# Moving four modulations of a hybrid encoder layer from the first FFN to the mLSTM, with DRAM parking and earlier query-weight loads

## The chip, the cores and the metric

One core of one Trainium2 chip runs the whole layer as a single program. The metric is the device time of one execution in microseconds; of several runs the median counts. TensorE (PE), VectorE (DVE), ScalarE (ACT), GpSimd (POOL) and SyncE (SP) work from queues of their own, in order; SP issues all DMA.

## The reference, cut to what matters

A layer of 1024 tokens by 1024 channels in float32, batch 1: FFN 1, a token mixer, FFN 2, each followed by a residual and a layer norm. A condition vector `c` gives nine modulation vectors of 1024 (shift, scale and gate for each of the three sub-layers; j = 3 * sub-layer + 0, 1, 2).

```python
mod = (silu(c) @ w_ada + b_ada).reshape(bsz, 3, 3, D_MODEL)
f1 = swiglu(modulate(x, mod[:, 0, 0], mod[:, 0, 1]), ffn1_w_up, ffn1_w_down)
x = post_norm(x, 0.5 * f1, mod[:, 0, 2], ln1_g, ln1_b)
tm = token_mixer(modulate(x, mod[:, 1, 0], mod[:, 1, 1]), ...)
x = post_norm(x, tm, mod[:, 1, 2], ln2_g, ln2_b)
f2 = swiglu(modulate(x, mod[:, 2, 0], mod[:, 2, 1]), ffn2_w_up, ffn2_w_down)
x = post_norm(x, 0.5 * f2, mod[:, 2, 2], ln3_g, ln3_b)
```

The mixer projects the tokens to queries, keys, values, output gates, input and forget gates (mLSTM, 4 heads, both directions, chunks of 128 tokens) and to the channels of an S5 state-space model. The mLSTM output is multiplied by the sigmoid of the output gate and normalised per head; the S5 output goes through a gated linear unit; one output projection takes both. So modulations 0 and 1 are needed at once, 2 at the end of FFN 1, 3 and 4 when the first norm is applied, 5 when the output projection is added to the residual, 6 and 7 at the norm after it, and 8 at the end of FFN 2.

## The kernel before

Activations lie channels by tokens, in tiles of 128x512: token half `h`, channel block `k`. All tiles come from a pool of 99 buffers named `s`; PSUM has 8 banks named `b`. Large products are made of three matmuls on operands split into a rounded and a remaining part (`mm3`, line 37); each split costs a cast and a subtraction. The FFN products use a scheme of seven block products, whose operands are combined on VectorE (`pair_jobs`, `product_jobs`), with the hidden rows kept in the DRAM tensors `Td`.

The order of work is made by a planner in Python while the program is built. Main work is a list of jobs on TensorE (`run_jobs`, line 602), whose weights come through a stream that loads up to ten chunks ahead (`Stream`, line 240). Everything else runs in lanes (line 371): generators that put operations into queues of 24, from which `issue` (line 540) takes whatever is ready by the planner's own clock, lanes in a fixed order, the lane `bg` last; each lane leaves some tiles of the pool free. A tile is taken when the operation that first writes it is issued, and a DMA into a tile is an operation like others. All DMAs go to SP's one queue, in the order in which they were planned.

Work around the change:

- `ada` (line 637) makes modulations from `w_ada`: for each j four steps of four loads of 256 KB, fetched a step ahead, and 16 products with 32-column weights (`cpad`), a copy of 256 columns, and for each two steps column sums with the vector `one`. Each of these float32 products leaves two records in the trace. j = 1 at the start is made on VectorE and ScalarE instead.
- `background` in `run` (line 2321), the lane `bg`: modulation 2, then 3 to 8, then the vectors that follow from them (`affine`, `cols`), then `s5_gen` (line 1380), which makes the S5 tables on VectorE and stores them to `Wd`, `Vd`, `Md` and last `Ed` (lines 1677 to 1695).
- `in_jobs` (line 1701): input projection; the last jobs are the values and the output gates, tokens by columns, into tiles of 128x4x128 (line 1775 for the gates, eight tiles that stay in the pool).
- `gates` (line 1829) makes the gate sequences of both directions, writes the running maxima to `Mr` (line 1890) and the query weights to `Wr` (line 1922).
- `mlstm` (line 2132), lane `lv`: for four pairs of chunks it loads `Mr` spread over 128 partitions (`load_m`, line 2149; a pair ahead), makes masked exponentials, and multiplies them with query-key products.
- `direction` (line 2195), lanes `l0` and `l1`: the chunk recurrence in each direction. Before chunk 1 and chunk 4 of a direction two loads of `Wr`, spread over partitions, come directly before the products that use them (lines 2204 to 2211).
- `finalize` (line 2268), lanes `fin0` to `fin3`: output gate (Tanh), per-head norm, transposes, for one chunk.
- `down_jobs` (line 957) in `mixer` (line 2300): the output projection in two halves of the rows, first the S5 channels in four passes of four units, then the mLSTM channels in passes of 8, 6 and 2. A unit is one 128x512 tile of the output; `fetch` loads the residual tiles `R` from `Xd` at the first half, and `evacuate` (line 1009) adds to them with the gate column `gcol[1]`. The 16 residual tiles stay in the pool between the halves.

Of the kernel before, what the change touches and what calls it, by code (L numbers as in the profile page):

```python
# [239 lines left out]
class Stream:  # L240
# [120 lines left out]
    def ensure(self, c):  # L361
        while self.ns <= min(c + AHEAD_SPLIT, len(self.chunks) - 1):
# [12 lines left out]
WINDOW = 24  # L375
U, Q = ("u0", "u1", "u2", "u3"), ("q2", "q3", "q0", "q1")
IN_ORDER = ([(x, 0) for x in U + ("g", "q2")] + [(x, 1) for x in U + ("g", "q2")]
# [18 lines left out]
class Kern:  # L396
    def __init__(self, ctx, tc, I, O, phases=("ffn1", "mixer", "ffn2")):
# [40 lines left out]
        self.Yd = dr.tile([4, 8, 16, 8, 128], F32, name="Yd")  # L438
        self.Mr = dr.tile([2, 4, S], F32, name="Mr")
        self.Wr = dr.tile([2, 4, S], F32, name="Wr")  # L440
# [515 lines left out]

    def down_jobs(self, w, rows, x, sub, passes, drain=(), after=None, fetch=None):

# [17 lines left out]
        for pi, units in enumerate(passes):  # L976
# [3 lines left out]
            for i, kt in enumerate(rows):  # L980
# [6 lines left out]
                def run(i=i, units=units, banks=banks, ys=ys, last=last, pi=pi):  # L987
                    if i == 0:
                        self.room(len(units))
                        banks.update({un: self.bank() for un in units})  # L990
                        if fetch:
                            for un in units:
                                fetch(*un)
                    ws = {y: st.get(idx[i, y]) for y in ys}
                    for un in units:
                        k, hh = un
                        wh, wl = ws[k // 4]
                        cc = slice(k % 4 * 128, k % 4 * 128 + 128)
                        mm3(nc, banks[un], wh[:, cc], wl[:, cc], *hsp[i, hh], i == 0, i == n - 1)
                        yield  # L1000
                    for hh in last:
                        del hsp[i, hh]
                    if i == n - 1:
                        self.later("ev", self.evacuate(sub, units, banks, after, pi))
                    yield

                self.jobs.append(Job(len(st.chunks) - 1, run, drain if pi == 0 and i == 0 else (), pre(i, sorted(new))))

    def evacuate(self, sub, units, banks, after, pi):
        for k, h in units:  # L1010
            self.add_to(sub, k, h, banks[k, h])
            self.free(banks[k, h])
            yield
        if after:
            after(pi)
# [685 lines left out]
    def in_jobs(self, drains):  # L1701
# [53 lines left out]
        def t_job(wi, h, k, c, banks):  # L1755
            def run():
# [10 lines left out]
                if k == KD - 1:  # L1767
                    for t in range(4):
                        if wi == 0:
                            x = self.S([128, 4, 129])  # L1770
                            P.memset(x[:, :, 128:129], 1.0)
                            self.v1[4 * h + t] = x
                            x = x[:, :, :128]
                        else:
                            x = self.o[4 * h + t] = self.S([128, 4, 128])
                        V.tensor_tensor(x, banks[t].rearrange("p (h x) -> p h x", h=4),
                                        bvo[wi].rearrange("p (h x) -> p h x", h=4), op=OP.add)
                    self.free(*banks)
                    if h:
# [49 lines left out]
    def gates(self):  # L1829
# [58 lines left out]
        for d in range(2):  # L1888
            for h in range(2):
                nc.sync.dma_start(self.Mr[d, :, h * 512:(h + 1) * 512], gm[h][RW[d]])  # L1890
        V.tensor_tensor(dc, mm, me, op=OP.subtract)
# [240 lines left out]
    def mlstm(self):  # L2132
# [16 lines left out]
        def load_m(c):  # L2149
            r = []  # L2150
            for d in range(2):
                mr = self.S([128, 4, 128])
                nc.sync.dma_start(mr, self.bc_ap(self.Mr, d * 4 * S + c * 128, [[0, 128], [S, 4], [1, 128]]))
                r.append(mr)
# [40 lines left out]
    def direction(self, d):  # L2195
# [3 lines left out]
        C = self.S([128, 2, 129])  # L2199
        qs = {}  # L2200
        for j in range(8):
            c = j if d == 0 else 7 - j
            hc, ts = self.tok(c)
            if j in (1, 4):
                for a in range(2):
                    x = qs[a] = self.S()
                    nc.sync.dma_start(x, self.bc_ap(self.Wr, (d * 4 + 2 * a) * S + hc * 512,
                                                    [[S, 2], [0, 64], [1, 512]]))
                    nc.any.tensor_tensor(x, x, qk[a, hc], op=OP.mult)
                del x  # L2210
                yield
            yield from self.wait(("vis", c))
            self.mark(("dir", d, j))
# [54 lines left out]
    def finalize(self, c):  # L2268
# [3 lines left out]
        while c not in self.o:  # L2272
            yield
        x, o, ng = self.cell.pop(c), self.o.pop(c), self.v["mlstm_norm_g"]
        nc.scalar.activation(o, o, AF.Tanh, scale=0.5)
# [24 lines left out]
    def mixer(self):  # L2300
# [8 lines left out]
        for n, first in enumerate((4, 0) if S5_FIRST else (0, 4)):  # L2309
            self.down_jobs(I["w_out"], range(first, first + 4), lambda i, h, f=first: self.rows(f + i, h), 1,  # L2310
                           self.END if n else self.QUARTERS, lanes[first == 0],
                           self.post(1, "ln2_g", "ln2_b", 2) if n else None, None if n else lambda k, h: self.fetch(self.Xd, k, h))

    def run(self):
# [6 lines left out]
        def background():  # L2321
# [3 lines left out]
            self.mark(("cols", 0))  # L2325
            yield from self.ada(range(3, 9))
            self.cpad = None
            self.affine(1, "ln1_g", "ln1_b")
            self.cols(1, False)
            self.affine(2, *(("ln2_g", "ln2_b") if mixer else ("ln1_g", "ln1_b")))  # L2330
            self.cols(2, True)
            for x in (("affine", 1), ("affine", 2), ("cols", 1), ("cols", 2)):
                self.mark(x)
            if mixer:
                yield from self.s5_gen()
                self.mark(("tables",))

# [91 lines left out]
```

## Time and profile before

| | us |
|---|---|
| Median of 3 runs | 1940.88 |
| Lowest and highest run | 1940.76, 1946.27 |
| Profiled execution, its own time | 1939.65 |
| Its span, first to last instruction | 1937.9 |
| TensorE busy in the span | 1847.2 |
| VectorE busy in the span | 1600.0 |
| ScalarE busy in the span | 648.2 |
| Mean granted TensorE clock, share of full speed | 0.982 |

Every operation is recorded at the helper's line 79, so groups are told apart by operation, tile and shape. In order of time: modulations and the first products (to about 165 us), the up products of FFN 1, its down products and the first norm (to about 820 us), input projection and S5 (to about 980 us), gated unit and mLSTM, the output projection's two halves (to about 1282 us), FFN 2.

### The profile page before, as it was taken

What the parts mean: (1) busy time and instruction counts of PE and PEld (TensorE: products, weight loads), DVE (VectorE), ACT (ScalarE), POOL (GpSimd) and SP (SyncE); (2) the same over time, 40 slices, a digit from 0 to 9 for tenths busy, and PEclk for the clock granted to TensorE, in tenths of its full rate; (3) what the DMA queues carried; (4) which work ended last, traced back from release to release, by engine and by line L of the source; (5) the groups of instructions that cost most, each with busy time, mean ns of one, the idle gap of its engine ahead of it and who ended that gap; (6) DMA issues with size and microseconds to landing.
All of it is one profiled execution on the core that took longest, in us unless ns stands there. A gap on an engine that the chain in (4) does not pass through costs nothing.

```text
span 1937.9 us, 29643 instructions
## 1 busy us (share of the span) xinstructions
PE 1847.2 (95%) x10544; PEld 1455.7 (75%) x10544; DVE 1600.0 (83%) x3351; ACT 648.2 (33%) x1201; POOL 200.6 (10%) x203
## 2 busy tenths in 40 slices
PE   5999999999999899999998899999999999999996
PEld 4767888777788677777776677678888888887775
DVE  7937889989899999879986796998677767597887
ACT  4512333333332326522253432542222222233412
POOL 0000000000000001110112311301111211000014
PEclk9999999999999989999999899999999999999998
DMA  9985233434493735482633430223232323574512
GB/s 325 313 300 192 82 110 116 158 132 141 150 343 113 262 129 196 159 271 73 207 104 93 150 97 11 77 91 121 84 121 95 109 82 109 179 256 143 184 44 76
DMA packets 187331, 290.54 MB, mean 150 GB/s; under 512 B 27024, under 2 KB 54800, under 8 KB 187184
## 3 DMA queue, kind: packets, MB, share of 16 engines
q1 hardware_dynamic: 187184, 288.65, 44.6%
q8 instruction: 83, 1.36, 0.3%
q14 instruction: 64, 0.52, 0.1%
HBM read 218.26 MB, written 70.32 MB: 149 GB/s over the span
## 4 chain that ended last, share of the span: by engine, by line
PE 79%; DVE 11%; DMA 5%; issue 3%; ACT 1%; SPq 0%; POOL 0%; DVEq 0%; ACTq 0%; POOLq 0%
PE b L79 79%; DVE s L79 10%; DMA s<-in_w_ada 2%; ACT s L79 1%; DMA s<-Wr 1%; DMA s<-in_x 1%; DVE er L79 0%; SPq L79 0%; DMA s<-in_glu_w 0%; DMA s<-in_w_first 0%; DVE lnv L79 0%; DMA s<-in_w_down 0%; DMA s<-Md 0%; DMA s<-Td 0%; POOL s L79 0%
## 5 line engine op out<-in xcount | busy, mean ns | idle before, releaser
L79 PE MATMUL b<-s 128*128 128x512 f32 (+5 forms) x9208 | 1817.6, 372 | 55.8 <-DVE s L79 37.1
L79 PEld LDWEIGHTS b<-s 128*128 128x128 f32 (+3 forms) x9208 | 1414.2, 176 | 428.2 <-DVE s L79 55.2
L79 DVE TENSOR_TENSOR s<-s 128x512 fp32r<-128x512 f32 (+5 forms) x1787 | 1003.0, 607 | 77.9 <-ACT s L79 23.6
L79 ACT ACTIVATE s<-s 128x512 fp32r<-128x512 f32 (+3 forms) x676 | 395.6, 625 | 567.3 <-DVE s L79 385.8
L79 DVE TENSOR_TENSOR s<-s,b 128x512 f32<-128x512 f32 (+1 forms) x340 | 215.4, 651 | 176.0 <-PE b L79 170.2
L79 POOL TENSOR_TENSOR s<-s 128x512 f32<-128x512 f32 (+1 forms) x116 | 170.6, 1485 | 1159.6 <-ACT s L79 478.1
L79 ACT ACTIVATE s<-b 128x512 f32<-128x512 f32 (+3 forms) x219 | 119.5, 553 | 479.9 <-PE b L79 446.2
L79 DVE CAST s<-s 128x512 fp32r<-128x512 f32 (+1 forms) x243 | 124.7, 516 | 8.5 <-DMA s<-in_x 3.1
L79 DVE SCALAR_TENSOR_TENSOR s<-b,gcol,s 128x512 f32<-128x512 f32 x56 | 39.5, 744 | 21.9 <-PE b L79 21.9
L79 ACT ACTIVATE s<-b,vec 128x128 f32<-128x128 f32 (+3 forms) x58 | 23.7, 464 | 94.2 <-PE b L79 81.5
L79 POOL MEMSET s<- 128x4 f32 (+3 forms) x57 | 6.0, 131 | 419.0 <-PE b L79 263.6
L79 PE MATMUL b<-ident,s 128*128 128x128 f32 (+1 forms) x208 | 31.5, 279 | 5.2 <-DVE s L79 5.2
L79 PEld LDWEIGHTS b<-ident,s 128*128 128x128 f32 (+1 forms) x208 | 24.9, 149 | 13.5 <-issue 7.7
L79 DVE TENSOR_TENSOR_SCAN s<-s 4x128 f32<-4x128 f32 (+1 forms) x48 | 32.9, 697 | 1.5 <-ACT s L79 0.9
L79 DVE SCALAR_TENSOR_TENSOR s<-s 128x320 f32<-128x320 f32 (+3 forms) x43 | 22.4, 529 | 4.1 <-ACT s L79 3.7
L79 ACT ACTIVATE s<-s,Bp,Gp 128x512 f32<-128x512 f32 x24 | 18.4, 803 | 20.6 <-DVE s L79 20.6
L79 ACT ACTIVATE s<-s,vec 128x512 f32<-128x512 f32 x28 | 20.9, 777 | 11.2 <-DVE s L79 11.1
L79 DVE SCALAR_TENSOR_TENSOR s<-s,vec 128x512 f32<-128x512 f32 (+1 forms) x36 | 24.1, 696 | 0.1
L79 ACT ACTIVATE s<-s,gcols 128x128 f32<-128x128 f32 x64 | 20.0, 391 | 2.7 <-POOL s L79 2.7
L79 PEld LDWEIGHTS b<-one,s 128*32 128x32 f32 x576 | 8.4, 113 | 15.8 <-DVE s L79 12.3
L79 PE MATMUL b<-one,s 128*32 128x1 f32 x576 | 9.2, 174 | 11.5 <-DVE s L79 11.5
L79 DVE SCALAR_TENSOR_TENSOR s<-s,gcol 128x512 f32<-128x512 f32 x24 | 18.8, 783 | 0.6
(102 smaller groups left out, 327.0 us busy)
## 6 DMA issues: line engine op xcount, KB each, us to landing
s<-in_w_up SPq DMA_DIRECT2D x170, 256.0 KB
s<-in_w_ada SPq DMA_DIRECT2D x144, 256.0 KB
Td<-s SPq DMA_DIRECT2D x140, 256.0 KB
s<-Td SPq DMA_DIRECT2D x140, 256.0 KB
s<-in_w_down SPq DMA_DIRECT2D x124, 256.0 KB
s<-in_x SPq DMA_DIRECT2D x32, 256.0 KB
Xd<-s SPq DMA_DIRECT2D x32, 256.0 KB
s<-in_w_vo SPq DMA_DIRECT2D x32, 256.0 KB
```

Of the source, the lines that this page charges most:

```text
L79: self.eng, self.alts, self.emit = eng, (), lambda: getattr(real, name)(*args, **kw)
```

## The change

It makes modulations 2, 3 and 4 as before, then the affine vectors of the first norm and the S5 tables, and modulations 5 to 8 only when the last S5 block (`("y", 7)`) has been made. Output gates are stored to a DRAM tensor `Od` and loaded again by `finalize`. After the first half of the output projection each residual tile is stored to `Xd` and given back; the second half fetches it again. The first two `Wr` loads of each direction are issued when its lane starts, the next two in its third step, ahead of their use in the fifth. `Mr` is laid out chunk by chunk, so that one partition reads 512 numbers in a row. The core of the diff:

```diff
+LATE = ("y", 7)
-        self.Mr = dr.tile([2, 4, S], F32, name="Mr")
+        self.Od = dr.tile([8, 128, 4, 128], F32, name="Od")
+        self.Mr = dr.tile([2, 8, 4, 128], F32, name="Mr")
...
-    def evacuate(self, sub, units, banks, after, pi):
+    def evacuate(self, sub, units, banks, after, pi, store):
         for k, h in units:
             self.add_to(sub, k, h, banks[k, h])
             self.free(banks[k, h])
+            if store:
+                self.nc.sync.dma_start(self.Xd[k * 128:(k + 1) * 128, h * HT:(h + 1) * HT], self.R[k][h])
+                self.R[k][h] = None
             yield
...
-                            x = self.o[4 * h + t] = self.S([128, 4, 128])
+                            x = self.S([128, 4, 128])
                         V.tensor_tensor(x, banks[t].rearrange("p (h x) -> p h x", h=4),
                                         bvo[wi].rearrange("p (h x) -> p h x", h=4), op=OP.add)
+                        if wi:
+                            nc.sync.dma_start(self.Od[4 * h + t], x)
+                            self.o[4 * h + t] = True
...
-                nc.sync.dma_start(self.Mr[d, :, h * 512:(h + 1) * 512], gm[h][RW[d]])
+                nc.sync.dma_start(self.Mr[d, 4 * h:4 * h + 4].rearrange("c h t -> h c t"),
+                                  gm[h][RW[d]].rearrange("h (c t) -> h c t", c=4))
...
-                nc.sync.dma_start(mr, self.bc_ap(self.Mr, d * 4 * S + c * 128, [[0, 128], [S, 4], [1, 128]]))
+                nc.sync.dma_start(mr, self.bc_ap(self.Mr, (d * 8 + c) * 512, [[0, 128], [128, 4], [1, 128]]))
...
-        qs = {}
+        qs, wr = {}, []
+
+        def load_w(hc):
+            for a in range(2):
+                wr.append(self.S())
+                nc.sync.dma_start(wr[a], self.bc_ap(self.Wr, (d * 4 + 2 * a) * S + hc * 512, [[S, 2], [0, 64], [1, 512]]))
+
+        load_w(d)
+        yield
         for j in range(8):
             c = j if d == 0 else 7 - j
             hc, ts = self.tok(c)
             if j in (1, 4):
                 for a in range(2):
-                    x = qs[a] = self.S()
-                    nc.sync.dma_start(x, self.bc_ap(self.Wr, (d * 4 + 2 * a) * S + hc * 512,
-                                                    [[S, 2], [0, 64], [1, 512]]))
-                    nc.any.tensor_tensor(x, x, qk[a, hc], op=OP.mult)
-                del x
+                    qs[a] = wr.pop(0)
+                    nc.any.tensor_tensor(qs[a], qs[a], qk[a, hc], op=OP.mult)
                 yield
+            if j == 2:
+                load_w(1 - d)
...
-        x, o, ng = self.cell.pop(c), self.o.pop(c), self.v["mlstm_norm_g"]
+        x, o, ng = self.cell.pop(c), self.S([128, 4, 128]), self.v["mlstm_norm_g"]
+        nc.sync.dma_start(o, self.Od[c])
         nc.scalar.activation(o, o, AF.Tanh, scale=0.5)
...
-                           self.post(1, "ln2_g", "ln2_b", 2) if n else None, None if n else lambda k, h: self.fetch(self.Xd, k, h))
+                           self.post(1, "ln2_g", "ln2_b", 2) if n else None, lambda k, h: self.fetch(self.Xd, k, h), not n)
...
-            yield from self.ada(range(3, 9))
+            yield from self.ada([3, 4])
+            self.affine(1, "ln1_g", "ln1_b")
+            self.mark(("affine", 1))
+            if mixer:
+                yield from self.s5_gen()
+                self.mark(("tables",))
+                yield from self.wait(LATE)
+            yield from self.ada(range(5, 9))
             self.cpad = None
-            self.affine(1, "ln1_g", "ln1_b")
             self.cols(1, False)
             self.affine(2, *(("ln2_g", "ln2_b") if mixer else ("ln1_g", "ln1_b")))
             self.cols(2, True)
-            for x in (("affine", 1), ("affine", 2), ("cols", 1), ("cols", 2)):
+            for x in (("affine", 2), ("cols", 1), ("cols", 2)):
                 self.mark(x)
-            if mixer:
-                yield from self.s5_gen()
-                self.mark(("tables",))
```

## Rows read from the trace of the kernel before

**Rows 1.** The page's first table, busy time by engine.

```profile
PE 1847.2 (95%) x10544; PEld 1455.7 (75%) x10544; DVE 1600.0 (83%) x3351; ACT 648.2 (33%) x1201; POOL 200.6 (10%) x203
```

**Rows 2.** The chain of waits, whole span: start us, us, what.

```profile
153.47 502.29 PE b L79 x2503
...
1053.98 19.44 DMA s<-Wr
```

**Rows 3.** Windows, FFN 1: us, PE, PEld, DVE, ACT, POOL, clock, DMA share, GB/s.

```profile
60.00:160.00 100.00, 97.97 (x1538) 68.86 (x1531) 58.60 (x112) 29.75 (x61) 7.21 (x4) 1.00 0.88 307
104.00:154.00 50.00, 47.97 (x717) 33.89 (x716) 10.35 (x18) 10.28 (x23) 2.98 (x2) 1.00 0.93 329
165.00:655.00 490.00, 490.00 (x2339) 390.77 (x2338) 447.01 (x1031) 162.86 (x289) 6.40 (x19) 1.00 0.46 153
655.00:680.00 25.00, 17.34 (x71) 13.63 (x70) 24.30 (x41) 7.35 (x12) 0.00 (x0) 0.91 0.81 286
```

**Rows 4.** Windows, mixer, columns as in rows 3.

```profile
976.00:1054.00 78.00, 77.53 (x380) 61.54 (x379) 64.24 (x110) 39.26 (x75) 19.86 (x19) 1.00 0.41 111
1054.00:1078.00 24.00, 11.14 (x51) 7.90 (x49) 8.49 (x29) 5.07 (x17) 0.00 (x0) 0.79 0.36 113
1078.00:1117.00 39.00, 35.18 (x292) 27.68 (x291) 35.80 (x121) 21.26 (x66) 16.45 (x17) 0.91 0.49 150
1117.00:1182.00 65.00, 61.58 (x341) 48.05 (x340) 59.62 (x294) 22.93 (x61) 6.22 (x6) 1.00 0.24 74
```

**Rows 5.** Groups by shape, whole span: busy us, mean ns, idle before.

```profile
L79 PE MATMUL b<-s 128*32 128x128 f32 x1024 | 40.1, 278 | 2.4 <-DMA s<-in_w_ada 1.9 <-issue 0.4
...
L79 DVE TENSOR_TENSOR s<-s,b 128x256 f32<-128x256 f32 x32 | 12.0, 410 | 0.0
```

**Rows 6.** Groups by shape, PE, 60 to 160 us.

```profile
L79 PE MATMUL b<-s 128*128 128x512 f32 x242 | 66.9, 412 | 0.0
L79 PE MATMUL b<-s 128*32 128x128 f32 x880 | 33.8, 278 | 2.0 <-DMA s<-in_w_ada 1.9
L79 PE MATMUL b<-one,s 128*32 128x1 f32 x416 | 5.8, 172 | 0.0
```

**Rows 7.** Groups by shape, PE, 170 to 300 us.

```profile
L79 PE MATMUL b<-s 128*128 128x512 f32 x562 | 130.5, 394 | 0.0
```

**Rows 8.** Timeline of SP's queue, a late store of the tables.

```profile
744.15 0.32 SPq L79 DMA_DIRECT2D Ed<-s  x1
```

**Rows 9.** Timeline of PE, FFN 1's down products, idle before in brackets.

```profile
677.60 32.94 PE L79 MATMUL b<-s 128*128 128x512 f32 x132 [7.66 <-DVE s L79]
715.30 11.75 PE L79 MATMUL b<-s 128*128 128x512 f32 x41 [4.76 <-DVE s L79]
```

**Rows 10.** Timeline of PE, a burst of modulation products.

```profile
141.34 0.43 PE L79 MATMUL b<-s 128*32 128x128 f32 x8 [0.45 <-DMA s<-in_w_ada]
```

**Rows 11.** Timeline of DVE, mLSTM, idle before in brackets.

```profile
1056.90 1.29 DVE L79 TENSOR_TENSOR s<-s 128x512 f32<-128x512 f32 x2 [8.06 <-DMA s<-Wr]
...
1062.11 0.69 DVE L79 TENSOR_TENSOR s<-s 128x512 f32<-128x512 f32 x1 [3.64 <-DMA s<-Wr]
...
1073.44 1.29 DVE L79 TENSOR_TENSOR s<-s 128x512 f32<-128x512 f32 x2 [8.86 <-DMA s<-Wr]
```

**Rows 12.** Timeline of SP's queue, mLSTM.

```profile
1006.35 23.20 SPq L79 DMA_DIRECT2D s<-in_w_out  x4
1031.54 11.65 SPq L79 DMA_DIRECT2D s<-Mr  x8
...
1047.56 1.19 SPq L79 DMA_DIRECT2D s<-Wr  x2
...
1053.37 5.80 SPq L79 DMA_DIRECT2D s<-Wr  x2
```

**Rows 13.** Windows of 5 us, mLSTM, columns as in rows 3.

```profile
1040.00:1045.00 5.00, 5.00 (x28) 3.89 (x27) 4.96 (x5) 2.73 (x6) 5.00 (x4) 1.00 0.86 208
1080.00:1085.00 5.00, 5.00 (x28) 4.14 (x28) 4.93 (x10) 0.28 (x1) 5.00 (x5) 0.51 0.48 125
```

**Rows 14.** Waits, whole span: total us, times, longest us.

```profile
ACT s L79 <- DMA s<-Td: 76.9, 34, 13.7
```

More of the change, by code (lines that the diff above doesn't have):

```diff
@@ L954, in pair_jobs, with down_jobs @@
             self.jobs.append(Job(cs[p], job(p), (("t", sub),) if f == NPLAIN[sub] and p == 0 else ()))
-    def down_jobs(self, w, rows, x, sub, passes, drain=(), after=None, fetch=None):
+    def down_jobs(self, w, rows, x, sub, passes, drain=(), after=None, fetch=None, store=False):
         nc, st = self.nc, self.st
@@ L1003, in run @@
                     if i == n - 1:
-                        self.later("ev", self.evacuate(sub, units, banks, after, pi))
+                        self.later("ev", self.evacuate(sub, units, banks, after, pi, store))
                     yield
                 self.jobs.append(Job(len(st.chunks) - 1, run, drain if pi == 0 and i == 0 else (), pre(i, sorted(new))))
-    def evacuate(self, sub, units, banks, after, pi):
+    def evacuate(self, sub, units, banks, after, pi, store):
         for k, h in units:
```

## The prediction

> **What bounds the kernel now.** I read the page's first table, then the chain of work that ended last, then windows by stage. The reader is to see that TensorE is busy for 1847.2 of 1937.9 us [rows 1]: whatever saves time must take TensorE work away from a stage that is full, or close one of the few gaps. The chain shows both kinds [rows 2]. From 153 us it stays on TensorE for 502.29 us, in the first FFN; near 1054 us it leaves TensorE for 19.44 us, to a load of `Wr` in the mLSTM.
>
> The windows say what each stage has to spare [rows 3]. From 60 to 160 us, where the modulations j = 2 to 8 run beside the first FFN products, PE is busy 97.97 of 100 us, and DMA at 0.88. From 165 to 655 us PE is busy all 490 us while VectorE is at 447.01. So in the first FFN each microsecond of modulation work on TensorE is a microsecond of the program.
>
> In the mixer [rows 4] the stretch from 976 to 1054 us is again full (77.53 of 78), 1054 to 1078 is half empty (11.14 of 24, clock 0.79), and the next two stretches lack 3.8 and 3.4 us. The sum is made against the profiled execution, 1939.65 us (1937.9 of span and 1.75 around it); the median of the runs, 1940.88, stands 1.23 above, and that is added at the end.
>
> **1. Four modulations leave the first FFN.** All 1024 records of the 32-column products belong to eight modulations (j = 0 and 2 to 8), 128 to each [rows 5]. Between 60 and 160 us there are 880 of them, their 416 column sums, and 242 records of 512 columns [rows 6]. What one of these 512-column records takes without company is 130 us / 562 = 0.231 us [rows 7], so the 242 account for 56.0 of 97.97 us, and 42.0 us are the price of 880/128 = 6.9 modulations: 6.1 us each, 24.4 for four. The 2.0 us that PE idled ahead of these records, 1.9 of it for `w_ada` [rows 6], go too.
>
> Does the stream use this time? Its cover would be gone if VectorE couldn't prepare the operands sooner, but from 104 to 154 us VectorE works 10.35 of 50 us [rows 3]. The 64 loads of 256 KB leave the same stretch, where DMA stands at 0.93, so weights don't come later. Modulations j = 2 to 4 stay. I take **-26.4** (between -20, if the stream now and then waits for its own operands, and -26.4).
>
> **2. The S5 tables start earlier.** Their generator ran behind all modulations in the same lane; now it follows j = 4. Its last products, those stored to `Ed`, run on until 744 us [rows 8], in a stretch where VectorE is the bound: 24.30 of 25 us busy from 655 to 680 [rows 3], and PE idles 7.66 and 4.76 us for it [rows 9]. The start moves by about four sevenths of 100 us, 57 us, and the FFN loses 26, so the generator gains some 30 us of lead, not 110: some of the table work leaves this stretch, not all. Between 0 and -12.4; I take **-5**, nearer to the end where VectorE stays full, since it is full here for its own work as well.
>
> **3. The same modulations arrive beside the mLSTM.** They wait for the last S5 block (its output goes out at 976 us) and must be through before the first output-projection results are scaled, for these read `gcol[1]`. Their instructions all count again: 512 product records, 256 column-sum records, 16 copies of 128x256 on ScalarE or VectorE, 64 DMAs on SP's queue.
>
> TensorE's price lies between two rows. In company it was 24.4 us. Eight product records that stand alone take 0.43 us [rows 10], a first one of 0.28 and seven more at 0.022; 128 at that rate and 64 column sums at 5.8/416 = 0.014 [rows 6] make 3.7 us, 14.7 for four, and if they also fill the 7.2 us of gaps left between 1078 and 1182 us, 7.5 remain. The company is 512-column work as before, so I take the first, less 4 us of gaps: **+20.4** (7.5 to 24.4). The copies are put on ScalarE or VectorE; a 128x256 operation took VectorE 0.41 us [rows 5], and ScalarE, busy 39.26 of 78 us there [rows 4], covers 16 of them.
>
> **4. The `Wr` wait.** VectorE, an in-order queue, stands 8.06, 3.64 and 8.86 us for these loads [rows 11]; queued behind are state updates, denominators and masks of both directions, so TensorE runs out. SP issued the loads at 1047.56 and 1053.37 us, the `Mr` loads at 1031.54, after it had been held for 23.20 us in four `w_out` loads [rows 12]. The change issues the first four `Wr` loads when the direction lanes open, and the other four two steps ahead. What is lost now: 12.86 us of PE idle in 1054 to 1078 us, and clock: 11.14 us at 0.79 and 35.18 us at 0.91 lose 2.3 and 3.2 us [rows 4]; TensorE had idled, and was granted 0.51 from 1080 to 1085 us, practically its 1.2 GHz level [rows 13]. Together 18.4. Bounds: 0, if the load still comes last, and -20.6, VectorE's whole wait. I take **-16**: the masks and denominators come next on VectorE, 35.80 of 39 us busy right after.
>
> `Mr` by chunk turns each partition's four runs of 512 bytes into one of 2 KB. Its loads are issued a pair ahead; no engine waits on `Mr` in the trace, so 0 in the sum, between 0 and -4. From 1040 to 1045 us, with `Mr` loads under way, DMA moved 208 GB/s at a share of 0.86, against 329 at 0.93 from 104 to 154 us [rows 3, 13]. The Trainium skill (DMA: Bandwidth & Descriptors, Specifications) puts line rate at runs of 512 bytes and up, by which the new order would move nothing; the rows speak against it in part, since these loads share the stretch with others. By the rule the term is 0, by the rows up to 4 us of earlier masks.
>
> **5. Parking.** Output gates: 8 stores and 8 loads of 256 KB; residual: 16 and 16. A gate's load is issued when its finalize step starts, and Tanh on ScalarE waits for it, with everything behind it. The nearest row is ScalarE's wait for `Td` loads, 76.9/34 = 2.26 us each [rows 14]: 18 us for eight. From 1117 to 1182 us ScalarE is busy 22.93 of 65, TensorE has the first half of the output projection to do [rows 4], so this is covered but for the last step or two: **+2** (0 to 18). The second fetch of the residual is issued when the second half opens and is wanted 96 matmuls, 22 us, later: 0. If SP were held, its cover would be gone and the adds would come late by the load's few microseconds. Stores wait for VectorE's add on SP, with FFN 2 weights behind them: 0, since SP has nothing due before them in that stretch, where DMA is at 0.24 [rows 4].
>
> **The sum:** -26.4 - 5 + 20.4 - 16 + 2 = -25.0; 1939.65 - 25.0 + 1.23 = **1916 us**.
>
> **Rivals.**
>
> *A, slower: SP's single queue.* The place is 976 to 1117 us. SP issues in order, and it has stood for 23.20 us on loads that wanted a free tile [rows 12]. If a modulation load waits so, `Mr` and `Wr` stand behind it. Eight loads in flight, 2.1 MB, take 6.4 us at the 329 GB/s of [rows 3]; once for each of four chunk pairs 25.6 us. With no gain at `Wr` and TensorE's full price: -26.4 + 24.4 + 25.6 = +23.6, 1964 us. It decides from 2 us a pair. The Trainium skill (DMA: Bandwidth & Descriptors, Anatomy of one DMA) has it that a semaphore wait happens on the issuing sequencer, before dispatch; by that rule every new parked store and every load without a tile holds what follows it. For it: 112 more issues in this stage. Against it: DMA at 0.41 and 0.36 [rows 4], so 16.8 MB fit in, and eight gate tiles come free. Chance 0.08.
>
> *B, no change.* The stage takes the modulations at full price, VectorE's chain replaces most of the `Wr` wait, tables give nothing: -26.4 + 24.4 - 4 + 4 (parking) = -2, 1939 us. For it speaks VectorE's load after 1078 us. Chance 0.10.
>
> *C, the loads aren't earlier.* The change wouldn't do what it says: the `Wr` loads stand on SP behind the same `w_out` loads. Everything but term 4 holds: -9, 1932 us. Chance 0.12.
>
> *D, it fits into the gaps.* Modulations +7.5, `Wr` -20.6, tables -12.4: -51.9, 1889 us. Against it: most gaps go with the `Wr` wait. Chance 0.12.
>
> **How the numbers follow.** The forecast has 0.58. Forecast, C and D are faster by over 0.3% (some 6 us, about what a measurement of this kernel can tell from no change): 0.82. B is the same, 0.10; A slower, 0.08. The range runs from 1896, which leaves out most of D, to 1940, which takes in B and C and leaves out A. The bounds of terms 3 to 5 lie within it unless several fall on one side.
>
> **What would show it.** No 32-column products of j = 5 to 8 before 165 us, and the TensorE-only piece of the first FFN over some 26 us sooner; `Ed` stores over well before 700 us; no wait of VectorE for `Wr` over 1 us; 976 us to the start of the output projection's second half (206 us now) within some 8 us of that in spite of 24 us more work. Wrong: waits of TensorE for `w_ada` or of ScalarE for `Od` of several microseconds each, or a clock under 0.9 between 976 and 1182 us.

## The result: 28 us slower, and where it went

The changed kernel takes 1969.34 us (median of 4 runs, 1964.66 to 1974.48) against 1941.04 (4 runs) of the kernel before: ratio 1.0136, 95% interval 1.0117 to 1.0155. The forecast, 1916 us and faster, was wrong, also in sign. The profiled run took 1968.95 us, its span 1967.1.

Three milestones that both traces have split the difference: the last `Xd` store of FFN 1, the last `Yd` store of S5, and the start of TensorE's long piece in FFN 2 on the chain.

| stretch | before, us | after, us | change | forecast |
|---|---|---|---|---|
| start to the last `Xd` store of FFN 1 | 820.4 | 783.7 | -36.7 | -31.4 |
| to the last S5 output store | 155.5 | 160.7 | +5.2 | 0 |
| to FFN 2's long TensorE piece | 305.2 | 367.3 | +62.1 | +6.4 |
| to the end | 656.8 | 655.4 | -1.4 | 0 |
| sum | 1937.9 | 1967.1 | +29.2 | -25.0 |

The rows behind the milestones, the kernel before and then the kernel after (stores on SP with first and last start; the chain's piece):

```profile
L79 SPq DMA_DIRECT2D Xd<-s x16: 319/327/412, 768.8 to 820.4; - x16
L79 SPq DMA_DIRECT2D Yd<-s x8: 320/323/364, 847.4 to 975.9; - x8
1281.13 498.55 PE b L79 x2149
```

```profile
L79 SPq DMA_DIRECT2D Xd<-s x16: 319/327/531, 733.4 to 783.7; - x16
L79 SPq DMA_DIRECT2D Yd<-s x8: 320/323/327, 815.5 to 944.4; - x8
1311.71 497.79 PE b L79 x2149
```

The first stretch came out as forecast, and a little better; the third took 62 us more, all of that gain and 25 us besides. The first table of the page answers to [rows 1]: TensorE is busy 8 of the 29 us more, for the same number of instructions, so it mostly idled longer.

```profile
PE 1855.4 (94%) x10544; PEld 1467.2 (75%) x10544; DVE 1595.1 (81%) x3345; ACT 654.0 (33%) x1209; POOL 191.8 (10%) x203
```

The chain of waits of the kernel after (start us, us, what), answering to [rows 2]: FFN 1's long piece begins at 51.93 instead of 153.47 us, as modulations j = 5 to 8 no longer interrupt it, and between 1047 and 1092 us two DMA waits stand where before there was one of 19.44.

```profile
51.93 456.43 PE b L79 x2697
...
1047.22 19.47 DMA s<-Wr
...
1076.16 15.59 DMA s<-Mr
```

Windows of the kernel after, columns as in rows 3. The first answers to [rows 3]: the modulation stretch is full, and DMA fell from 0.93 to 0.35. The others lie in the mixer of [rows 4].

```profile
104.00:154.00 50.00, 50.00 (x217) 40.56 (x216) 40.38 (x145) 13.89 (x24) 0.00 (x0) 1.00 0.35 121
...
976.00:1054.00 78.00, 67.22 (x416) 52.68 (x408) 28.96 (x56) 22.68 (x52) 13.59 (x14) 0.92 0.50 165
...
1050.00:1060.00 10.00, 2.19 (x5) 1.80 (x6) 1.58 (x5) 3.12 (x11) 0.00 (x0) 0.50 0.23 85
1060.00:1070.00 10.00, 5.25 (x29) 4.04 (x29) 4.30 (x15) 1.76 (x5) 2.59 (x3) 0.67 0.36 107
1090.00:1100.00 10.00, 3.32 (x60) 3.03 (x64) 4.90 (x14) 6.86 (x22) 8.19 (x8) 0.50 0.67 205
```

TensorE idles there and its granted clock is 0.50, the 1.2 GHz level, in what little it does. SP's queue in the same stretch (start us, us, operation, count) answers to [rows 12]:

```profile
1040.86 2.41 SPq L79 DMA_DIRECT2D Od<-s  x4
1043.36 8.90 SPq L79 DMA_DIRECT2D s<-Wr  x4
1052.37 7.60 SPq L79 DMA_DIRECT2D s<-Mr  x4
1060.32 15.73 SPq L79 DMA_DIRECT2D s<-Wr  x4
1076.16 7.72 SPq L79 DMA_DIRECT2D s<-Mr  x4
1083.97 24.58 SPq L79 DMA_DIRECT2D s<-in_w_ada  x16
```

The `w_ada` loads stand last; what holds the queue are the eight `Wr` loads themselves. VectorE, then GpSimd, on their timelines (idle before in brackets; VectorE answers to [rows 11]):

```profile
1050.80 0.69 DVE L79 TENSOR_TENSOR s<-s 128x512 f32<-128x512 f32 x1 [4.79 <-DMA s<-Wr]
1056.06 0.69 DVE L79 TENSOR_TENSOR s<-s 128x512 f32<-128x512 f32 x1 [4.50 <-DMA s<-Wr]
1061.71 0.69 DVE L79 TENSOR_TENSOR s<-s 128x512 f32<-128x512 f32 x1 [4.83 <-DMA s<-Wr]
1066.72 0.69 DVE L79 TENSOR_TENSOR s<-s 128x512 f32<-128x512 f32 x1 [3.99 <-DMA s<-Wr]
```

```profile
1067.41 5.39 POOL L79 TENSOR_TENSOR s<-s 128x512 f32<-128x512 f32 x4 [17.91 <-DMA s<-Mr]
...
1091.81 5.38 POOL L79 TENSOR_TENSOR s<-s 128x512 f32<-128x512 f32 x4 [14.04 <-DMA s<-Mr]
```

VectorE gets one load of 256 KB every 5.0 to 5.7 us, although SP had issued the first four by 1052.26 us. The DMA view of the kernel after, 1064 to 1074 us (busy share in tenths and GB/s in 40 slices, packets, the queue's share of 16 engines), says why:

```profile
DMA  1111111111111111111111111111141111111111
GB/s 49 49 49 49 57 49 57 49 49 49 49 49 49 49 49 49 49 49 49 49 49 49 57 49 49 57 49 49 49 115 49 49 49 49 49 57 49 49 57 41
DMA packets 257, 0.52 MB, mean 52 GB/s; under 512 B 11, under 2 KB 11, under 8 KB 256
...
q1 hardware_dynamic: 256, 0.50, 13.1%
```

A constant 49 GB/s at 13.1% of sixteen engines is what two of them (12.5%) would show. The packets of the trace say the same: nearly always two packets of 2 KB are under way at a time, each for 84 ns, and 2 x 2 KB in 84 ns are 49 GB/s. The same view of the kernel *before*, 1058 to 1068 us, showed this too, around its own `Wr` waits:

```profile
DMA  1121111111111111111111111111444334344114
GB/s 49 57 82 49 49 57 49 49 49 49 49 49 49 49 49 49 49 49 49 49 49 49 49 57 49 49 49 55 135 145 135 135 125 141 111 125 152 51 57 137
```

A `Wr` load has the source pattern `[[S, 2], [0, 64], [1, 512]]`: two rows, each repeated over 64 partitions. The Trainium skill (DMA: Bandwidth & Descriptors, Why a DMA increments its semaphore by 16 and not by 1, "How many engines") says that a DMA is spread over the largest number of engines up to 16 that divides the slowest dimension of both its patterns. By that rule a `Wr` load gets two engines; the trace agrees, with 13.1% and two packets at a time.

### The profile page after: what moved, and what is told of

The parts are those of the page before. It is cut to its first block, busy times and chain, and to the rows that moved or that the text cites. A ratio compares the mean times of both kernels' runs of the same rounds, so it can differ in the third digit from the quotient of the medians.

```text
span 1967.1 us, 29743 instructions
## 1 busy us (share of the span) xinstructions
PE 1855.4 (94%) x10544; PEld 1467.2 (75%) x10544; DVE 1595.1 (81%) x3345; ACT 654.0 (33%) x1209; POOL 191.8 (10%) x203
## 4 chain that ended last, share of the span: by engine, by line
PE 82%; DVE 11%; DMA 4%; issue 1%; ACT 1%; SPq 0%; POOL 0%; DVEq 0%; POOLq 0%; ACTq 0%
PE b L79 82%; DVE s L79 10%; DMA s<-Mr 1%; DMA s<-Wr 1%; ACT s L79 1%; DMA s<-Vd 1%; DMA s<-in_w_ada 1%; DVE er L79 0%; DMA s<-in_x 0%; SPq L79 0%; DMA s<-in_w_first 0%; POOL s L79 0%; DVE lnv L79 0%; DMA s<-Td 0%; DMA Ud<-s 0%
## 5 line engine op out<-in xcount | busy, mean ns | idle before, releaser
L79 PE MATMUL b<-s 128*128 128x512 f32 (+6 forms) x9208 | 1825.6, 374 | 80.0 <-DVE s L79 42.9
L79 DVE TENSOR_TENSOR s<-s 128x512 fp32r<-128x512 f32 (+6 forms) x1789 | 1000.4, 606 | 85.4 <-ACT s L79 41.7
L79 DVE TENSOR_TENSOR s<-s,b 128x512 f32<-128x512 f32 (+2 forms) x340 | 214.4, 653 | 188.7 <-PE b L79 170.0
L79 POOL TENSOR_TENSOR s<-s 128x512 f32<-128x512 f32 (+2 forms) x114 | 161.7, 1435 | 1230.9 <-DVE s L79 433.7
L79 DVE CAST s<-s 128x512 fp32r<-128x512 f32 x244 | 122.9, 507 | 8.2 <-DMA s<-in_x 3.4
L79 DVE SCALAR_TENSOR_TENSOR s<-b,gcol,s 128x512 f32<-128x512 f32 x56 | 39.7, 744 | 27.1 <-PE b L79 27.1
L79 DVE TENSOR_TENSOR s<-b,s 128x512 f32<-128x512 f32 x16 | 10.5, 685 | 23.7 <-PE b L79 23.7
L79 ACT ACTIVATE s<-s,Bp,Gp 128x512 f32<-128x512 f32 x26 | 20.3, 805 | 28.1 <-DVE s L79 28.1
L79 ACT ACTIVATE s<-s,gcols 128x128 f32<-128x128 f32 x64 | 20.4, 392 | 17.4 <-POOL s L79 17.4
L79 ACT ACTIVATE s<-s,vec 128x512 f32<-128x512 f32 x27 | 20.3, 778 | 0.7 <-DVE s L79 0.6
```

What stands on the lines that cost most here:

```text
L79: self.eng, self.alts, self.emit = eng, (), lambda: getattr(real, name)(*args, **kw)
```

## The experiments

Theory Q: the `Wr` loads are slow in themselves, by their outer dimension of two, and block SP's queue. Theory T: the mixer pays for the moved modulations what FFN 1 gains, as it was first put because they take tiles of the pool. Theory P: the modulations' TensorE time is simply not hidden.

**e1 and e2: each `Wr` load cut by partitions**, in the changed kernel and in the kernel before. Bytes and order stay.

```diff
-                nc.sync.dma_start(wr[a], self.bc_ap(self.Wr, (d * 4 + 2 * a) * S + hc * 512, [[S, 2], [0, 64], [1, 512]]))
+                for p in range(2):
+                    nc.sync.dma_start(wr[a][p * 64:p * 64 + 64],
+                                      self.bc_ap(self.Wr, (d * 4 + 2 * a + p) * S + hc * 512, [[0, 64], [1, 512]]))
```

> The changed kernel, with each spread load of Wr cut in two loads of 64 partitions. Theory Q (the Wr loads are slow in themselves: VectorE got four of them 4.6 to 5.7 us apart, and now eight stand in SP's queue ahead of the Mr loads, which come 14 and 18 us late): the four waits of VectorE for Wr and the two long waits of GpSimd for Mr go, the idle and slow-clock time of TensorE between 1045 and 1110 us (some 34 us) mostly closes, and the time falls to 1935 to 1948 us. Theory T (the modulations take the tiles of the pool from the gated unit, so that TensorE has nothing else to do in the mLSTM) expects less than 8 us of gain, 1961 us or more. Theory P (the modulations' TensorE time is simply not hidden) expects no gain.

> The kernel before, with the same cut of each spread Wr load and nothing else. Theory Q: the three waits of VectorE for Wr, 20.6 us, shrink to under 6 us and the time falls by 8 to 16 us, to 1925 to 1933 us. If the wait came from SP's queue alone (the loads are issued late, whatever their shape), it stays at 1938 to 1944 us.

e1: 1930.65 us, ratio to the kernel before 0.9935 (0.9911 to 0.9959). That is 39 us off the changed kernel and 4 us below theory Q's range; T, as put with the tiles, expected under 8 us of gain and P none, and both fall. e2: 1933.89, 0.9942 (0.9923 to 0.9961). SP's queue in e1, and the queue's share in its DMA view from 1037.5 to 1043 us:

```profile
1037.84 4.96 SPq L79 DMA_DIRECT2D s<-Wr  x8
1042.91 2.20 SPq L79 DMA_DIRECT2D s<-Mr  x4
1045.15 2.38 SPq L79 DMA_DIRECT2D s<-Wr  x4
```

```profile
q1 hardware_dynamic: 773, 1.31, 76.2%
```

Eight half loads go by in 4.96 us, where four whole ones took 8.90 and 15.73. VectorE's wait for `Wr` falls from 18.1 to 1.9 us, and from 1050 to 1060 us TensorE is busy 8.86 of 10 us at full clock, against 2.19 at 0.50. In the kernel before the same cut gives 11 us, as Q expected, and VectorE's wait for `Wr` falls from 20.6 to 7.9 us with the loads at their old place.

**e5: the same loads cut by columns**, so as many and as small, but each with its outer dimension of two.

```diff
-                    nc.sync.dma_start(wr[a][p * 64:p * 64 + 64],
-                                      self.bc_ap(self.Wr, (d * 4 + 2 * a + p) * S + hc * 512, [[0, 64], [1, 512]]))
+                    nc.sync.dma_start(wr[a][:, p * 256:p * 256 + 256],
+                                      self.bc_ap(self.Wr, (d * 4 + 2 * a) * S + hc * 512 + p * 256, [[S, 2], [0, 64], [1, 256]]))
```

> The changed kernel; each spread Wr load cut in two by columns (2 x 64 partitions x 256 numbers each), so there are as many and as small loads as in the run that cut it by partitions (e1, 1930.7 us), but each keeps its outer dimension of two. Theory Q (the outer dimension of two makes the load slow, whatever its length): VectorE still waits more than 15 us for Wr and GpSimd more than 40 us for Mr, no gain or a few us: 1955 to 1972 us. Rival (smaller loads in larger number are what helped): as e1, 1928 to 1935 us, and the waits nearly gone.

1953.9 us, 1.0061 (1.0045 to 1.0077): 1 us under the range of theory Q and far from e1. VectorE waits 20.5 us for `Wr`, as Q has it, and GpSimd 37.0 for `Mr`, a little under the 40 it expected. Its DMA view from 1043 to 1054 us is Q's too:

```profile
DMA  1111111111111111111111111111111111111111
...
q1 hardware_dynamic: 454, 0.46, 13.4%
```

The order of work says how far this goes. In their traces e1 and e5 have the same operations in the same order on VectorE, ScalarE, GpSimd and SP, and on TensorE but for four neighbouring records. So what lies between them, some 24 us (1.0061 against 0.9935), is neither order nor size nor number. The runs of e5 are 1 KB long instead of 2, but its packets take 46 ns instead of 84, nearly in proportion; what is left is the outer dimension, which keeps two packets under way instead of many. The changed kernel departs from that order from 1049 us on: given eight more loads, the planner arranged the mLSTM differently. Its loads are no slower than e5's (49 GB/s against 42), so the other 15 us of e1's 39 (1.0136 against 1.0061) come from the order or from the loads' size and number; which of them was not separated.

**e6: the slow loads back at their old place**, all else as changed.

```diff
-        load_w(d)
-        yield
...
                 for a in range(2):
+                    if a == 0:
+                        load_w(hc)
                     qs[a] = wr.pop(0)
...
-            if j == 2:
-                load_w(1 - d)
```

> The changed kernel, but the slow Wr loads issued where the kernel before issues them, directly ahead of the products that use them; nothing else is undone. Theory Q with order (a slow load hurts by what stands behind it on SP, and the change put Wr ahead of Mr): GpSimd's waits for Mr fall from 60 us to under 25, VectorE's for Wr rise to 20 us as in the kernel before, total 1950 to 1962 us. Rival (it is their length alone, the order doesn't matter): 1966 to 1973 us, as the change.

1965.04 us, 1.0122 (1.0097 to 1.0147): the interval overlaps that of the changed kernel, and the time is 1 us under the rival's range and 3 above that of Q with order. The waits moved as expected (GpSimd for `Mr` 21.2 us instead of 38.4, VectorE for `Wr` 27.6 instead of 18.1), the time didn't. So the loads' place on SP, which I had made part of theory Q, makes no difference that these runs can tell.

**e9: issuing the loads ahead, alone**, in the kernel before: term 4 by itself.

> The kernel before with one part of the change: the Wr loads issued when a direction's lane opens and in its third step, loads uncut. The prediction on record gives this part -16 us: 1925 us. Theory Q (a load with an outer dimension of two is slow in itself, so an earlier place gains only what lies between the old and the new place on SP, and Mr comes later): within 8 us of the kernel before, 1934 to 1950 us, with Wr or Mr waits of 10 us and more left.

1945.21 us, 0.9996 (0.9985 to 1.0008): no change. SP's `Wr` issues in e9, and the last ones of the kernel before:

```profile
1044.89 12.43 SPq L79 DMA_DIRECT2D s<-Wr  x4
1078.05 16.21 SPq L79 DMA_DIRECT2D s<-Wr  x4
```

```profile
1077.02 15.28 SPq L79 DMA_DIRECT2D s<-Wr  x4
```

The first come 2.7 us sooner than the 1047.56 of [rows 12], behind the same `w_out` loads (23.20 us) and the eight `Mr` loads, and the last four 1 us later: planned earlier, the loads hardly are earlier. Waits of e9 from 964 to 1290 us (total us, times, longest):

```profile
POOL s L79 <- DMA s<-Wr: 30.1, 3, 17.8
DVE s L79 <- DMA s<-Wr: 18.3, 3, 8.4
```

The loads are still what both engines wait for.

**e3 and e4: the changed kernel without the move, and the move alone** in the kernel before. Only the generator `background` is exchanged.

> The changed kernel with the background lane as before, so modulations 3 to 8 and then the tables; parking, the early Wr loads and the order of Mr stay changed. Theory Q: slower than before or the same, 1938 to 1955 us, since the Wr loads are still long and still ahead of Mr. Theory T and theory P: without the modulations in the mLSTM the early loads help, 1920 to 1932 us.

> The kernel before with the background lane of the change only: four modulations and the tables moved, no parking, Wr and Mr as before. Theory Q: the first FFN's gain of some 31 us stays and the mixer pays some 24 to 40 us, 1930 to 1950 us. Theory T: tiles are tighter still without parking, the mixer pays 60 us or more, 1965 us or more. Theory P: 1935 to 1945 us.

e3: 1937.72 us, 0.9959 (0.9945 to 0.9974), between the ranges of Q and T. e4: 1957.16, 1.0066 (1.0042 to 1.0089), outside all three ranges. The move alone costs about 12 us, the rest gains about 7, and together they cost 28: the parts don't add up. e3 is e9 with parking and `Mr` by chunk, and faster than it by some 7 us, clear of the intervals; which of the two gives this was not tested. e4's chain of waits goes over `Wr` for 18.50 and 9.77 us and over `w_ada` for 10.76.

**e7: quick loads, no move**, which beside e1 prices the move.

> The changed kernel with quick Wr loads (cut by partitions) and the modulations j = 5 to 8 and the tables back at their old place. Beside e1 (1930.7 us) it prices the move alone. Prediction on record: the move gives -26.4 - 5 + 20.4 = -11, so 1941 us here. Theory T (the mixer pays for the modulations all that FFN 1 gains, in TensorE work, tiles of the pool and VectorE work): 1926 to 1934 us, the same as e1 within a few us, with the last S5 store some 32 to 36 us later than in e1.

1933.17 us, 0.9958 (0.9941 to 0.9974), against e1's 0.9935: the intervals overlap, as T expected in its wider form. (The profiled execution of e7 took 1927.24 us, 6 under the median.) The last S5 store is at 975.7 us, in e1 at 939.6, 36.1 sooner, and none of it is left at the end. From that store to FFN 2's long piece e7 takes 292.2 us and e1 331.9. TensorE's products of 512 columns in this stretch, in e7:

```profile
L79 PE MATMUL b<-s 128*128 128x512 f32 x880 | 218.0, 403 | 10.1 <-DVE s L79 4.6 <-ACT s L79 3.8 <-POOL s L79 1.5
```

The same and the modulations' own, in e1:

```profile
L79 PE MATMUL b<-s 128*128 128x512 f32 x941 | 238.3, 410 | 11.7 <-DVE s L79 6.0 <-ACT s L79 2.8 <-POOL s L79 2.3
L79 PE MATMUL b<-s 128*32 128x128 f32 x512 | 19.7, 285 | 2.6 <-issue 2.4
...
L79 PE MATMUL b<-one,s 128*32 128x1 f32 x256 | 3.9, 171 | 0.4 <-ACT s L79 0.4
```

The modulations' 768 records take 23.6 us, close to the forecast's 20.4. The other part was in no term: 61 more products of 512 columns lie behind the last S5 store, which with them take 20.3 us more (some 15 for the 61 at e7's 0.248 us each, the rest because each takes longer). They had run before it: e1 has 16 fewer ahead of the last `Xd` store and 46 fewer between the two stores, within one at the borders. S5 itself didn't get shorter: from 850 to 900 us of e1 VectorE is busy 48.22 of 50 us and TensorE only 39.67, in e7 TensorE 48.36. So part of FFN 1's lead was work put off, and its place was left idle. TensorE's idle time behind the store is the same in both (17.8 and 17.7 us). Which products are put off, and why, was not settled.

**e8 and e13: the modulations beside FFN 1's down products** instead of the mLSTM, with quick and with slow loads; all else as changed.

```diff
-LATE = ("y", 7)
+LATE = ("down", 0)
```

> The changed kernel with quick Wr loads; the modulations j = 5 to 8 start once the first down products of FFN 1 are under way (after the S5 tables) instead of after the last S5 block. Theory T (beside the mLSTM the modulations cost more than beside FFN 1's down products, whose gaps and idle DMA they can use): under 1930 us, 1915 to 1928. Rival (a modulation costs its 6 us of TensorE wherever TensorE is full): 1930 to 1936 us.

> The changed kernel with the Wr loads left as they are (uncut, slow) and only the modulations j = 5 to 8 moved, to the place beside FFN 1's down products (as e8). Theory F (slow Wr loads cost what TensorE lacks in other work meanwhile: with the modulations beside the mLSTM only 22 products of 512 columns lie between 1040 and 1120 us, with them elsewhere 85 to 118): close to e8, 1916 to 1928 us, with SP's Wr loads still several us each and over 80 products of 512 columns in the 80 us around them. Rival (a slow load a step ahead costs some 39 us in this kernel wherever the modulations are): 1945 us or more.

e8: 1916.94 us, 0.9871 (0.9852 to 0.9890), faster than both kernels. TensorE in e8, 600 to 705 us: the 512 modulation products cost the same 19.9 us here. Ahead of the two groups of [rows 9], which showed 7.66 and 4.76, VectorE lets TensorE idle 1.82 and 1.30 us.

```profile
670.51 4.85 PE L79 MATMUL b<-s 128*128 128x512 f32 x69 [1.82 <-DVE s L79]
...
708.40 9.78 PE L79 MATMUL b<-s 128*128 128x512 f32 x41 [1.30 <-DVE s L79]
```

```profile
L79 PE MATMUL b<-s 128*128 128x512 f32 x326 | 84.0, 406 | 1.9 <-DVE s L79 1.8
L79 PE MATMUL b<-s 128*32 128x128 f32 x512 | 19.9, 284 | 1.0 <-DMA s<-in_w_ada 1.0
```

The last `Xd` store is 13.0 us sooner than in e7 (806.2 against 819.2 us); from 600 us up to it TensorE idles 5.2 us for VectorE, in e7 15.0; the tables are done earlier there (VectorE is busy 80.2 us from 600 to 705 us, in the kernel before 100.9). Behind the last S5 store lie 880 wide products, as in e7, so nothing is put off past it.

e13: 1922.08 us, 0.9876 (0.9839 to 0.9912), not told apart from e8, although its loads are as slow as ever (SP's `Wr` issues, ns min/median/max):

```profile
L79 SPq DMA_DIRECT2D s<-Wr x8: 480/2752/6639, 1024.1 to 1066.0; - x8
```

What differs from the changed kernel is what TensorE has to do meanwhile. Groups of wide products in 80 us around the loads, e13 from 1026 to 1106 us and the kernel after from 1040 to 1120:

```profile
L79 PE MATMUL b<-s 128*128 128x512 f32 x87 | 22.2, 402 | 0.0
```

```profile
L79 PE MATMUL b<-s 128*128 128x512 f32 x22 | 7.7, 516 | 7.9 <-ACT s L79 7.9
```

These are the products that TensorE got through, so a stall makes them fewer as well: in one and the same order e1 gets through 68 in such a window (1035 to 1115 us) and e5 through 40. By the order alone, between the first and the last of the chunk products with 129 columns, stand 99 wide products in e8 and e13, 30 in e1 and e5, and 12 in the changed kernel.

All the cases side by side (ratio to the kernel before):

| rest of the change in all | modulations in FFN 1, early | beside the down products | beside the mLSTM |
|---|---|---|---|
| slow `Wr` loads | 0.9959 (e3) | 0.9876 (e13) | 1.0136 (the change); 1.0061 in e1's order (e5) |
| quick `Wr` loads | 0.9958 (e7) | 0.9871 (e8) | 0.9935 (e1) |

In each of the first two columns the order is the same on all engines but SP, and no loss by slow loads is measured; the intervals leave room for some 4 us (e3) and 8 us (e13), and in the traces the third stretch is 13.3 us longer in e3 than in e7 (whose traced execution lies 6 us under its median) and 7.0 in e13 than in e8. Beside the mLSTM slow loads cost 24 us at the same order. Neither they nor the modulations alone make the kernel slower than before with the rest of the change in (e3, e13; e1). That the thin order is what makes them dear is argued, not shown: the kernel before has 96 wide products there and loses some 11 us to its slow loads (e2, whose order is a little different). How the order comes to be so thin beside the mLSTM was not taken apart.

**e10, e11, e12: parking and the layout of `Mr`**, on e8. e10 keeps the residual tiles; e11 the gate tiles too; e12 has the old `Mr`.

```diff
-                           self.post(1, "ln2_g", "ln2_b", 2) if n else None, lambda k, h: self.fetch(self.Xd, k, h), not n)
+                           self.post(1, "ln2_g", "ln2_b", 2) if n else None, None if n else lambda k, h: self.fetch(self.Xd, k, h))
```

> Run e8 (modulations beside FFN 1's down products, quick Wr loads; 1916.9 us) without parking the residual between the halves of the output projection. In e8 ScalarE waited 23.1 us once for an Od load that stood on SP behind stores of the residual. Theory P (that wait costs TensorE time): the wait falls under 5 us and the time by 3 to 8 us, to 1909 to 1914 us. Rival (TensorE has the first half of the output projection to do meanwhile, as the prediction said: parking +2): the wait goes or moves, and the time stays within 3 us, 1914 to 1920 us.

> As e10, and the output gates stay in their tiles too (no Od). The mixer then has no more DMA than the kernel before but the cut Wr loads. If the tiles that parking frees matter without modulations in that stage, 1920 to 1930 us, with w_out loads on SP waiting for tiles as in the kernel before (23.20 us); if they don't, 1910 to 1920 us.

> Run e8 with Mr in its old layout (each of 128 partitions reads four runs of 512 bytes instead of one of 2 KB). The prediction gave the layout 0, between 0 and -4: so 1917 to 1921 us here, and SP's Mr loads no more than 1 us longer each. Rival (short runs are slow, as spread loads were for Wr): Mr loads of several us each and waits of GpSimd for Mr, 1925 us or more.

Ratios 0.9867 (0.9847 to 0.9887), 0.9864 (0.9841 to 0.9887) and 0.9872 (0.9852 to 0.9892): none differs from e8. e8's wait for a parked gate, 964 to 1260 us, is gone in e10, and the time is the same:

```profile
ACT s L79 <- DMA s<-Od: 23.4, 2, 23.1
```

Theory P of e10 (that this wait costs TensorE time) falls; other work covers the wait, as the forecast had it. In e11 the `w_out` loads hold SP 23.21 us as in [rows 12], also without effect. In e12 the first eight `Mr` loads hold SP 12.52 us, in e8 5.06, nearly 1 us more each:

```profile
1019.87 12.52 SPq L79 DMA_DIRECT2D s<-Mr  x8
```

```profile
1020.59 5.06 SPq L79 DMA_DIRECT2D s<-Mr  x8
```

One issue took 4.18 us, more than the expectation's 1 us allows.

## Why the prediction was wrong, by its own steps

**Terms 1 and 2 (FFN 1, tables)** held together: -36.7 us measured against -31.4. On TensorE's timeline the long group ahead of the 132 products of [rows 9] ends at 645.90 us instead of 669.94: 24.0 sooner, within term 1's bounds. The other 12.7 lie behind it, where the tables were to give -5, at most -12.4; some 4 us of them are 16 of the put-off products (2974 before the last `Xd` store, 2958 after; 0.24 us each). `Ed` stores end at 628.6 us instead of 744.1.

**Term 3 (modulations beside the mLSTM)** was right in the price of their own records, 23.6 us in e1 against +20.4, within its bounds (26.9 in the changed kernel, where the clock is lower). The sum lacked the 61 wide products that moved with them and the S5 stretch that got no shorter (+5.2).

**Term 4 (`Wr`) is the step that failed.** The prediction took a `Wr` load for an ordinary one of 256 KB that came late, because SP had been held by `w_out` loads, put the bounds at 0 and -20.6, and left out a loss. Two things in that were wrong. The load runs at some 50 GB/s on two engines, 5 us each, so that most of the wait is the load itself (e2: 7.9 us are left of 20.6). And the change doesn't make it earlier: in e9 SP reaches it 2.7 us sooner, and in the changed kernel 99.0 us behind the last S5 store instead of 71.7. The term alone is worth 0 (e9). The rows that said so were in the trace of before: [rows 12] has SP at two `Wr` loads for 5.80 us, and the DMA view a flat 49 GB/s. The prediction read only averages of longer windows (113 GB/s, 0.36 in [rows 4]).

The third stretch, step by step through the traces: 305.2 us before; 292.2 in e7 (quick loads, parking and layout, no move), -13.0; 331.9 in e1 (the move), +39.7 where term 3 had +20.4; 353.9 in e5 (slow loads, the same order), +22.0; 367.3 in the changed kernel (whole loads, another order), +13.4. These steps add up to 62.1 whatever they mean, and e7's trace lies 6 us under its median, so each is good to a few us. But they place the miss against +6.4: some 19 us belong to term 3 (39.7 against 20.4) and some 38 to term 4 (22.4, the steps without the move, against -16), less the 2 of parking.

**`Mr` by chunk**: 0 in the time, as forecast, beside quick loads (e12). But of the two readings the rows' was the better one for the loads: runs of 512 bytes held SP 2.5 times as long as runs of 2 KB. The Trainium skill (DMA: Bandwidth & Descriptors, Specifications) puts both at line rate; these are issue times, and no run here shows the two rates.

**Term 5 (parking)**: 0 against +2, covered as said, beside quick loads (e10, e11). With whole `Wr` loads parking and layout together gave some 7 us (e3 against e9).

**Rivals.** A came within 6 us of the time, by another mechanism: no long wait goes back to modulation loads, and TensorE's weight loads waited 1.1 us for `w_ada` in that stage. SP was held all the same, by the `Wr` loads and by parking: it stands 13.0 us for VectorE's sums ahead of the `Od` stores at 1040.86 us, with the first `Wr` loads right behind. What that place on SP is worth stays open; e6 and e9 show nothing for it. C, that the loads aren't earlier, came true in its condition, in e9 as it was written, behind `w_out`, and in the changed kernel behind the `Od` stores; its time failed by the rest. B and D fell. Of the signs named, the two for FFN 1 came; "no wait of VectorE for `Wr` over 1 us" failed (four of 4 to 5), as did the 206 us of the mixer; of the signs against, the low clock came (0.86 from 976 to 1182 us), and the waits for `w_ada` and `Od` didn't.

## What to carry to other kernels

Before moving a load that is waited for, look at its own rate: a DMA view with a flat, low GB/s and a share near 2/16 says that the load's shape is the limit, and then cut it along its partitions instead of issuing it earlier; and see in the trace whether a load that was planned earlier is earlier at all. A stage's filler work is part of its price: work moved into a stage can drive out of it the work that covered a wait there, and parts that are harmless alone (slow loads in e3, modulations in e1) can then cost dearly together. Put moved work where the bounding engine idles and DMA has room, here beside the down products (DMA at 0.50 from 600 to 705 us before, 0.94 in e8; e8 is 25 us faster than before, of which e7 has 8 without the move).

## What the runs showed of the hardware that was not expected

The outer dimension of these loads' pattern sets their rate: 52 GB/s at 13.1% of the DMA engines with two rows spread over 64 partitions each, 237 GB/s at 76.2% once each load holds one row (from 1037.5 to 1043 us of e1, other transfers among them). Cutting by columns left 42 GB/s at 13.4%. A packet of 2 KB takes 84 ns (median) in both cases; what differs is how many are under way at once, two in the changed kernel from 1064 to 1069 us and up to some sixteen in e1.
